# One-core transformer blocks on Trainium2: the recurrence's gates in three fp32r passes, its two directions at two places of a head

## The chip, the cores and the metric

The kernel runs on one NeuronCore of a Trainium2 chip. The engines meant here are TensorE (PE, matmuls), VectorE (DVE), ScalarE (ACT, with function tables that an ACT_TABLE_LOAD exchanges) and SyncE (SP, which issues the DMAs). Each works off its own queue of instructions in order; semaphores make one wait for another. The metric is the device time of one launch in microseconds, smaller is better.

## What is computed

Two transformer blocks follow each other. The first (a gated delta rule, a spatial gating and a mixture of experts) is not touched. The second mixes tokens by grouped-query attention and, beside it, by a bidirectional gated linear recurrence, both over 512 tokens and 16 meta tokens (528 columns); gates of tanh form weigh the two and are added, and a feed-forward layer follows. The part that the change concerns is the recurrence, here for one direction:

```python
def rg_lru(xc, wa, ba, wx, bx, lam, reverse):
    xb = xc.reshape(B, T, RNN_BLOCKS, RNN_BLOCK)          # 8 blocks of 128 channels
    r = sigmoid(einsum('btnc,ncd->btnd', xb, wa) + ba)
    i = sigmoid(einsum('btnc,ncd->btnd', xb, wx) + bx)
    log_a = RG_C * r * log_sigmoid(lam)
    a = exp(log_a)
    u = sqrt(-expm1(2.0 * log_a)) * (i * xc)
    # h[t] = a[t] * h[t-1] + u[t], backwards in time if reverse
```

`xc` is a projection of the tokens after a convolution over four of them. So for each block of 128 channels there are four products of a 128x128 weight with 528 columns: two gates, `rg` and `ig`, in two directions `d`.

## The kernel before

The second block's loop (L1552 on) runs over eight heads `n`, and in each it computes attention head `n` and the recurrence's block `n` together. A head has these pieces, written as generators of which `next` runs one stage:

- `gates` (L2028): three dense products of 128 channels by 512 tokens into a `psA` buffer, 24 matmuls of 128x512 each, called ga, rn and gr here after what they write (ga and rn by a tanh, gr as the GELU factors `grx`, `gry`).
- `attention`: the weights of four query tiles, two at a time, each six matmuls of 264 columns into a `psD` buffer; DVE's maximum `m` (TENSOR_REDUCE), ACT's exponential `pr` with its sum `s`, DVE's normalisation (L2111); then `turned` transposes two tiles on PE: 16 columns into a free part of the same `psD` buffers (L2117), 512 into `psB` (L2122), split into `PThi` by ACT and `PTlo` by DVE. The product with the values comes a head later (`next(a0)`) and gives `ao`.
- `rnn_x` (L1984): 48 matmuls of 264 columns for the next head's projection `xr`, and its convolution `xc` on DVE. It also issues the DMAs of the gates' weights `wg`, one head ahead.
- `rnn_gates` (L2013): the four products in fp32, eight matmuls of 264 columns (L2023) into `psD` tiles, a sigmoid of ACT each, and `ig*xc` on DVE (L2026).
- `rnn`: of the head before, on ACT and DVE only: `th` (tanh, then `th<-a,th` of DVE, L2069), the exponential of `rg`, a square root, `ig<-ig,th` (L2075) and the scan (L2078) for each direction, then the sum of the directions and `ao`.

An fp32 matmul shows as two records in the trace, one in the format fp32r as one. The dense products, weights and projections already use three fp32r passes (`mm3`, L190 to L192): a value is split into a high part, rounded to fp32r by an ACT copy, and the rest, by a DVE subtraction (`split`, L162), and high by high, high by rest and rest by high are added up. Their columns are read `by_turns`: a half's columns are taken from its first and second half alternately, and `unturned` when the result is read.

PE's order is that of the code, by hand (L1549). The tile scheduler orders ACT's and DVE's instructions, and their order is fixed in the built program. In heads 1 to 6 PE's order is: ga, the product with the values of the head before, the gates of both directions, weights of tiles 0 and 1, rn, `turned`, gr, weights of tiles 2 and 3, `rnn_x` of the next head, `turned`. In head 7 the product with the values stands between the two directions. PSUM holds two buffers each of `psA`, `psB` and `psD`; gates and attention weights share `psD`. The pool of `rg`, `ig`, `xr`, `xc` and `wg` has two buffers of each; the scans of head n-1 run during head n, ahead of the gates of n+1, which take over their `rg` buffer.

Of the kernel before, what the change touches and what calls it, by code (L numbers as in the profile page):

```python
# [9 lines left out]
FT = mybir.dt.float32  # L10
FR = mybir.dt.float32r
I32 = mybir.dt.int32
BF = mybir.dt.bfloat16
AF = mybir.ActivationFunctionType
# [44 lines left out]
def by_turns(x):  # L59

    return x.rearrange("p (s c) -> p c s", s=2)
# [14 lines left out]
class Net:  # L76
# [1443 lines left out]
    def block2(self, rctx, pctx):  # L1520
        nc, I = self.nc, self.I
        T = META + S
        h = self.res
        octx = ExitStack()
        self.wraw = self.pool(octx, "wraw", 4, side="right")
        bp = self.pool(octx, "b2c", side="right")
        self.h2_d = self.dr.tile([NT, 128, D], FT, name="h2_d")
        self.q_d = self.dr.tile([NH, 128, S], FT, name="q_d")
        with ExitStack() as ctx:
            gp = self.pool(ctx, "kv", side="right")  # L1530
            kv = self.kv_tiles(gp)
            xctx = ctx.enter_context(ExitStack())
            xp = self.pool(xctx, "xn", side="right")
            xT = (xp.tile([128, NK, T], FR, name="xn_hi"), xp.tile([128, NK, T], FR, name="xn_lo"))
            with ExitStack() as c:
                vec, cl = self.vec2, self.cl
                self.norm_kvq(c, h, xT, kv, gp)
            rctx.close()
            ga, rn = ([gp.tile([128, S], FT, name=f"{m}{n}") for n in range(NK)] for m in ("ga", "rn"))
            self.whl = self.pool(xctx, "whl", 2, side="right")  # L1540
            pctx.close()
            pctx = ExitStack()
            self.psums(pctx, 2, 2, 2)
            w_out = I["w_out_2"][0]
            mix = []
            with ExitStack() as c:
                rp = self.pool(c, "rnl", 2)
                tp = self.pool(c, "atl", 2)
                c.enter_context(self.tc.manual_schedule(engines={mybir.EngineType.PE}))  # L1549
                x = self.rnn_x(rp, 0, vec, xT)  # L1550
                a0 = st0 = old = None
                for n in range(NK):  # L1552
                    a = self.attention(tp, n, kv, rn, ga, gp, mix)
                    g = self.gates(rp, n, xT, rn, ga)
                    if n + 1 < NK:
                        next(g)
                        if n:
                            next(a0)
                        st = self.rnn_gates(rp, n, vec, x)
                        if old:  # L1560
                            next(old)
                        next(g)
                        next(a)
                        next(g)
                        next(a)
                        next(g)
                        if n:
                            r0 = self.rnn(rp, n - 1, cl, st0, rn)
                            next(r0)
                        next(a)  # L1570
                        if n + 1 < NK:
                            x = self.rnn_x(rp, n + 1, vec, xT)
                        next(g)
                        if n + 1 < NK:
                            next(a)
                        if n:
                            next(r0)
                            old = a0
                    else:
                        next(g)  # L1580
                        st = self.rnn_gates(rp, n, vec, x, lambda: next(a0))
                        next(old)
                        next(g)
                        next(a)
                        next(g)
                        next(a)
                        if n:
                            r0 = self.rnn(rp, n - 1, cl, st0, rn)
                            next(r0)
                        next(a)  # L1590
                        next(g)
                        next(g)
                        if n + 1 < NK:
                            x = self.rnn_x(rp, n + 1, vec, xT)
                        if n + 1 < NK:
                            next(a)
                        if n:
                            next(r0)
                        if n:
                            next(a0)  # L1600
                    a0, st0 = a, st
                for _ in self.rnn(rp, n, cl, st, rn):
                    pass
                pd = None
                pss = []
                for k in range(0, NK, 2):
                    if k == 2:
                        next(a0)
                        next(a0)
                    hi, lo = self.wchunk(w_out, k * 128, 2, 0, 512)  # L1610
                    if k == 0:
                        next(a0)
                        for _ in range(2):
                            pd = self.psD.tile([128, 2, 512], FT, name="psD")
                            pss += [pd[:, 0, :], pd[:, 1, :]]
                    for t in range(NT):
                        self.tm_step(pss[t], hi, lo, mix, k, TOKS[t], NK)
            xctx.close()
            h = self.pool(octx, "hB").tile([128, NT, D], FT, name="hB")
            for t in range(NT):  # L1620
                nc.sync.dma_start(h[:, t, :], self.h2_d[t])
            for t in range(NT):
                nc.vector.tensor_tensor(h[:, t, :512], h[:, t, :512], pss[t], OP.add)
            pctx.close()
            hT, first = self.mix_out(octx, ctx, mix, h)
        with ExitStack() as ctx:
            self.ffn(ctx, h, hT, first)
        octx.close()
# [353 lines left out]
    def rnn_x(self, p, n, vec, xT):  # L1982

        nc, I = self.nc, self.I  # L1984
        T = META + S
        H = T // 2
        nhi, nlo = xT
        wg = p.tile([128, 2, 2, 128], FT, name="wg")
        nc.sync.dma_start(wg[:, 0], I["rg_wa_2"][0, :, n].rearrange("d c e -> c d e"))
        nc.sync.dma_start(wg[:, 1], I["rg_wx_2"][0, :, n].rearrange("d c e -> c d e"))  # L1990
        hi, lo = self.wchunk(I["w_in_2"][0], 0, NK, 1536 + n * 128, 128)
        xr = p.tile([128, T + 3], FT, name="xr")
        nc.vector.memset(xr[:, 0:2], 0.0)
        nc.vector.memset(xr[:, T + 2:], 0.0)
        for j in range(2):
            js = slice(j * H, (j + 1) * H)
            ps = self.psA.tile([128, 512], FT, name="psA")
            for k in range(NK):
                self.mm3(ps[:, :H], hi[:, k, :], lo[:, k, :], by_turns(nhi[:, k, js]), by_turns(nlo[:, k, js]),
                         k == 0, k == NK - 1)  # L2000
            self.act(halves(xr[:, 2 + j * H:2 + (j + 1) * H]), unturned(ps[:, :H]), AF.Copy)
        c = p.tile([128, T], FT, name="xc")
        nc.vector.tensor_scalar(c, xr[:, 0:T], vec[:, n:n + 1], vec[:, 32 + n:33 + n], op0=OP.mult, op1=OP.add)
        for j in range(1, 4):
            nc.vector.scalar_tensor_tensor(c, xr[:, j:j + T], vec[:, 8 * j + n:8 * j + n + 1], c,  # L2005
                                           op0=OP.mult, op1=OP.add)
        return c, wg

    def rnn_gates(self, p, n, vec, x, meanwhile=lambda: None):

        nc = self.nc
        T = META + S
        H = T // 2  # L2013
        c, wg = x
        rg = p.tile([128, 2, T], FT, name="rg")
        ig = p.tile([128, 2, T], FT, name="ig")
        for d in range(2):
            if d:
                meanwhile()
            for w, dst, bias in ((0, rg, 40), (1, ig, 56)):  # L2020
                ps = self.psD.tile([128, 2, 512], FT, name="psD")
                for j in range(2):
                    nc.tensor.matmul(ps[:, j, :H], wg[:, w, d, :], c[:, j * H:(j + 1) * H], start=True, stop=True)  # L2023
                self.act(dst[:, d, :].rearrange("p (a b) -> p a b", a=2), ps[:, :, :H], AF.Sigmoid,
                         bias=vec[:, bias + 8 * d + n:bias + 8 * d + n + 1])
        nc.vector.tensor_tensor(ig, ig, c[:, None, :].to_broadcast([128, 2, T]), OP.mult)  # L2026
        return rg, ig

    def gates(self, p, n, xT, rn, ga):

# [279 lines left out]
```

## Time and profile before

| | |
|---|---|
| time, median of three runs | 1963.28 us (1961.18 to 1964.82) |
| profiled run, time / span | 1958.82 / 1957.0 us |
| mean granted clock of TensorE | 0.977 |
| busy, share of span: PE / DVE / ACT | 1804.4 (92%) / 994.8 (51%) / 706.7 (36%) |
| the eight heads' loop: first weights of head 0 to those of head 7 | 1292.86 to 1534.75 us |

The shares are means over the two blocks and the experts; what a change in the heads' loop is worth is read there, from the timeline of each engine. In a timeline row stand the start, the busy time, engine, line, operation, output and inputs, shapes and the count of like instructions that the row joins; in brackets the idle time ahead of it and what ended that.

### The profile page before, as it was taken

To read this page: it belongs to the slowest core of one execution; us is meant where nothing else is said; L and a number is where in the kernel's file an instruction comes from. 1 tells how busy PE (TensorE), PEld (TensorE's weight loads), DVE (VectorE), ACT (ScalarE), POOL (GpSimd) and SP (SyncE) were. 2 spreads that over 40 slices of the span, in tenths; PEclk is the share of its full clock that TensorE was granted. 3 is DMA by queue.
4 is the path that set the end of the run, shared out by engine and by line. 5 is a ranking of instruction groups with operands and counts; after the bars stand their busy time and mean duration, and the time that the engine had idled before them with its cause. 6 is when DMAs were issued, how large, how long until landed. Compare 5 with 4: busy or idle time off the path is not lost. (4 is left out here: it accounts for less than half of the span.)

```text
span 1957.0 us, 23667 instructions
## 1 busy us (share of the span) xinstructions
PE 1804.4 (92%) x9193; PEld 1340.7 (69%) x9193; DVE 994.8 (51%) x1856; ACT 706.7 (36%) x1156; POOL 18.7 (1%) x30
## 2 busy tenths in 40 slices
PE   6899899879999879998889887999999999999999
PEld 5787578767889733443333334888888778888887
DVE  6743577763546622222212238756887863333333
ACT  5232443423333512111101016456767743323332
POOL 0000000000000000000000000000000000000000
PEclk9899999999999979999999998999999999999999
DMA  8636767596558499999999975332221243333231
GB/s 257 97 88 114 107 76 86 119 159 95 98 179 303 176 412 425 426 425 425 425 425 426 376 307 186 119 119 71 81 75 55 66 128 97 97 107 98 98 129 65
DMA packets 255716, 372.64 MB, mean 190 GB/s; under 512 B 30386, under 2 KB 196819, under 8 KB 231667
## 3 DMA queue, kind: packets, MB, share of 16 engines
q1 hardware_dynamic: 245666, 345.94, 56.7%
q10 hardware_dynamic: 7632, 16.78, 2.2%
q0 software_dynamic: 2304, 8.39, 1.1%
q8 instruction: 73, 1.20, 0.2%
q14 instruction: 41, 0.33, 0.1%
HBM read 349.03 MB, written 22.04 MB: 190 GB/s over the span
## 5 line engine op out<-in xcount | busy, mean ns | idle before, releaser
L90 ACT ACTIVATE whi<-raw 128x1024 fp32r<-128x1024 f32 (+1 forms) x203 | 234.2, 1158 | 470.3 <-PE psA L191 291.0
L162 DVE TENSOR_TENSOR wlo<-raw,whi 128x1024 fp32r<-128x1024 f32 (+1 forms) x195 | 249.0, 1278 | 256.9 <-ACT whi L90 239.9
L1267 PE MATMUL psB<-mwt,XT 128*64 128x512 f32 x1008 | 234.5, 600 | 15.0 <-ACT XT L90 9.0
L192 PE MATMUL psA<-hT_hi,wlo 128*128 128x512 f32 (+1 forms) x456 | 177.7, 390 | 16.4 <-DVE wlo L162 16.4
L1267 PEld LDWEIGHTS psB<-mwt,XT 128*64 128x64 f32 x1008 | 74.0, 138 | 163.3 <-issue 137.9
L190 PE MATMUL psA<-hT_hi,whi 128*128 128x512 f32 (+1 forms) x456 | 178.4, 391 | 0.9 <-ACT whi L90 0.9
L191 PE MATMUL psA<-hT_lo,whi 128*128 128x512 f32 (+1 forms) x456 | 178.4, 391 | 0.0
L1332 DVE TENSOR_TENSOR res<-res,psA 128x512 f32<-128x512 f32 x128 | 79.3, 679 | 115.2 <-PE psA L1327 115.2
L1300 PE MATMUL psB<-mwt,hbT 128*64 128x512 f32 x480 | 117.1, 596 | 21.5 <-DMA mwt<-in_w 20.1
L191 PE MATMUL psA<-hn_lo,whi 128*128 128x512 f32 (+1 forms) x368 | 136.3, 370 | 0.3 <-DVE hn_lo L2174 0.3
L190 PE MATMUL psA<-hn_hi,whi 128*128 128x512 f32 (+1 forms) x368 | 136.4, 371 | 0.2 <-ACT hn_hi L90 0.2
L192 PE MATMUL psA<-hn_hi,wlo 128*128 128x512 f32 (+1 forms) x368 | 136.2, 370 | 0.0
L1276 DVE TENSOR_TENSOR sl<-sl,psB 128x512 f32<-128x512 f32 x16 | 11.0, 688 | 204.8 <-PE psB L1267 204.8
L190 PE MATMUL psA<-xn_hi,whi 128*128 128x512 f32 (+1 forms) x320 | 109.4, 342 | 0.4 <-ACT qx L90 0.4
L192 PEld LDWEIGHTS psA<-hT_hi,wlo 128*128 128x128 f32 (+1 forms) x456 | 87.0, 191 | 32.2 <-DVE wlo L162 18.2
L192 PE MATMUL psA<-xn_hi,wlo 128*128 128x512 f32 (+1 forms) x320 | 108.2, 338 | 0.0
L191 PE MATMUL psA<-xn_lo,whi 128*128 128x512 f32 (+1 forms) x320 | 108.1, 338 | 0.0
L1300 PEld LDWEIGHTS psB<-mwt,hbT 128*64 128x64 f32 x480 | 36.2, 136 | 96.7 <-issue 57.4
L191 PEld LDWEIGHTS psA<-hT_lo,whi 128*128 128x128 f32 (+1 forms) x456 | 87.1, 191 | 20.4 <-issue 8.4
L190 PEld LDWEIGHTS psA<-hT_hi,whi 128*128 128x128 f32 (+1 forms) x456 | 87.3, 191 | 17.3 <-issue 3.4
L90 ACT ACTIVATE hbT<-psA 128x512 f32<-128x512 f32 x16 | 9.6, 597 | 238.8 <-PE psA L1284 238.8
L190 PEld LDWEIGHTS psA<-hn_hi,whi 128*128 128x128 f32 x368 | 69.5, 189 | 9.5 <-ACT hn_hi L90 0.5
(569 smaller groups left out, 3459.8 us busy)
## 6 DMA issues: line engine op xcount, KB each, us to landing
mwt<-in_w SPq DMA_DIRECT2D x188, 1024.0 KB, 20.7
raw<-in_w_in SPq DMA_DIRECT2D x108, 512.0 KB, 7.6
raw<-in_w_ffn_in SPq DMA_DIRECT2D x44, 512.0 KB, 3.9
raw<-in_w_ffn_out SPq DMA_DIRECT2D x22, 512.0 KB, 3.6
raw<-in_w_pa SPq DMA_DIRECT2D x8, 512.0 KB, 4.2
raw<-in_w_pb SPq DMA_DIRECT2D x8, 512.0 KB, 4.2
raw<-in_w_o SPq DMA_DIRECT2D x8, 512.0 KB, 6.9
raw<-in_w_out SPq DMA_DIRECT2D x8, 512.0 KB, 3.6
```

The source lines that it names most:

```text
L90: ins = self.nc.scalar.activation(out, in_, func, **kw)
L162: self.nc.vector.tensor_tensor(lo, x, hi.bitcast(FT), OP.subtract)
L190: nc.tensor.matmul(out, whi, xhi, start=first, stop=False)
L191: nc.tensor.matmul(out, whi, xlo, start=False, stop=False)
L192: nc.tensor.matmul(out, wlo, xhi, start=False, stop=last)
L1267: nc.tensor.matmul(ps[CAP * i:CAP * (i + 1), :], XT[:, r0 + k, CAP * i:CAP * (i + 1)], w_, start=(r0 + k == 0), stop=(r0 + k == NK - 1))
L1276: nc.vector.tensor_tensor(so, so, h[1], OP.mult)
L1300: nc.tensor.matmul(pys[half][CAP * i:CAP * (i + 1), :], hT[:, r0 + k, CAP * i:CAP * (i + 1)], ws[i][:, k, half * 512:(half + 1) * 512], st ...
L1332: nc.vector.tensor_tensor(x, x, unturned(ps), OP.add)
```

## The change

`rnn_x` now splits the gates' weights (`wghi`, and the rest into a buffer of `wg`) and the convolved columns (the high part into an `xr` buffer, the rest `xclo`): two more ACT copies and two more DVE subtractions in a head. `rnn_gates` becomes a generator: each product is three fp32r passes on columns by turns, 24 matmuls of 264 columns a head in place of eight in fp32, and the sigmoid puts the columns back in order. Its first stage, direction 0, stays where the gates stood. Its second, direction 1 with the multiplication by `xc`, moves in heads 0 to 6 behind `turned` of tiles 0 and 1 and ahead of gr. In head 7 the order stays. `xc`, `wghi` and `xclo` get one buffer each. Lines below L2000 move by up to 12.

```diff
--- before.py
+++ after.py
@@ -1556,13 +1556,15 @@
                         next(g)
                         if n:
                             next(a0)
-                        st = self.rnn_gates(rp, n, vec, x)
+                        rg = self.rnn_gates(rp, n, vec, x)
+                        st = next(rg)
                         if old:
                             next(old)
                         next(g)
                         next(a)
                         next(g)
                         next(a)
+                        next(rg)
                         next(g)
                         if n:
                             r0 = self.rnn(rp, n - 1, cl, st0, rn)
@@ -1578,7 +1580,10 @@
                             old = a0
                     else:
                         next(g)
-                        st = self.rnn_gates(rp, n, vec, x, lambda: next(a0))
+                        rg = self.rnn_gates(rp, n, vec, x)
+                        st = next(rg)
+                        next(a0)
+                        next(rg)
                         next(old)
                         next(g)
                         next(a)
@@ -1988,6 +1993,8 @@
         wg = p.tile([128, 2, 2, 128], FT, name="wg")
         nc.sync.dma_start(wg[:, 0], I["rg_wa_2"][0, :, n].rearrange("d c e -> c d e"))
         nc.sync.dma_start(wg[:, 1], I["rg_wx_2"][0, :, n].rearrange("d c e -> c d e"))
+        ws = p.tile([128, 2, 2, 128], FR, name="wghi", bufs=1), p.tile([128, 2, 2, 128], FR, name="wg")
+        self.split(*ws, wg)
         hi, lo = self.wchunk(I["w_in_2"][0], 0, NK, 1536 + n * 128, 128)
         xr = p.tile([128, T + 3], FT, name="xr")
         nc.vector.memset(xr[:, 0:2], 0.0)
@@ -1999,32 +2006,37 @@
                 self.mm3(ps[:, :H], hi[:, k, :], lo[:, k, :], by_turns(nhi[:, k, js]), by_turns(nlo[:, k, js]),
                          k == 0, k == NK - 1)
             self.act(halves(xr[:, 2 + j * H:2 + (j + 1) * H]), unturned(ps[:, :H]), AF.Copy)
-        c = p.tile([128, T], FT, name="xc")
+        c = p.tile([128, T], FT, name="xc", bufs=1)
         nc.vector.tensor_scalar(c, xr[:, 0:T], vec[:, n:n + 1], vec[:, 32 + n:33 + n], op0=OP.mult, op1=OP.add)
         for j in range(1, 4):
             nc.vector.scalar_tensor_tensor(c, xr[:, j:j + T], vec[:, 8 * j + n:8 * j + n + 1], c,
                                            op0=OP.mult, op1=OP.add)
-        return c, wg
-
-    def rnn_gates(self, p, n, vec, x, meanwhile=lambda: None):
+        cs = p.tile([128, T + 3], FR, name="xr")[:, 0:T], p.tile([128, T], FR, name="xclo", bufs=1)
+        self.split(*cs, c)
+        return c, cs, ws
+
+    def rnn_gates(self, p, n, vec, x):
 
         nc = self.nc
         T = META + S
         H = T // 2
-        c, wg = x
+        c, (chi, clo), (whi, wlo) = x
         rg = p.tile([128, 2, T], FT, name="rg")
         ig = p.tile([128, 2, T], FT, name="ig")
         for d in range(2):
-            if d:
-                meanwhile()
             for w, dst, bias in ((0, rg, 40), (1, ig, 56)):
                 ps = self.psD.tile([128, 2, 512], FT, name="psD")
                 for j in range(2):
-                    nc.tensor.matmul(ps[:, j, :H], wg[:, w, d, :], c[:, j * H:(j + 1) * H], start=True, stop=True)
-                self.act(dst[:, d, :].rearrange("p (a b) -> p a b", a=2), ps[:, :, :H], AF.Sigmoid,
+                    js = slice(j * H, (j + 1) * H)
+                    self.mm3(ps[:, j, :H], whi[:, w, d, :], wlo[:, w, d, :], by_turns(chi[:, js]), by_turns(clo[:, js]),
+                             True, True)
+                self.act(dst[:, d, :].rearrange("p (a s c) -> p a s c", a=2, s=2),
+                         ps[:, :, :H].rearrange("p a (c s) -> p a s c", s=2), AF.Sigmoid,
                          bias=vec[:, bias + 8 * d + n:bias + 8 * d + n + 1])
+            if d == 0:
+                yield rg, ig
         nc.vector.tensor_tensor(ig, ig, c[:, None, :].to_broadcast([128, 2, T]), OP.mult)
-        return rg, ig
+        yield
 
     def gates(self, p, n, xT, rn, ga):
 
```

ACT in a head, from the end of rn to grx, before (`th`, `rg`, `a` belong to `rnn`; `whi` is a weight's high part):

```order
L90 ACTIVATE rn_8942<-psA 128x512
L90 ACTIVATE PThi<-psD 16x128 x2
L90 ACTIVATE PThi<-psB 128x4x128 x2
L90 ACTIVATE th<-rg,cl 128x528
L90 ACTIVATE rg<-rg,cl 128x528
L90 ACTIVATE th<-rg,cl 128x528
L90 ACTIVATE a_9878<-rg 128x528
L90 ACTIVATE rg<-rg,cl 128x528
L90 ACTIVATE a_9883<-rg 128x528
L90 ACTIVATE whi<-raw 128x1024
L90 ACTIVATE grx<-psA 128x512
```

And after:

```order
L90 ACTIVATE rn_8942<-psA 128x512
L90 ACTIVATE PThi<-psD 16x128 x2
L90 ACTIVATE PThi<-psB 128x4x128 x2
L90 ACT_TABLE_LOAD
L90 ACTIVATE rg<-psD,vec_5881 128x528
L90 ACTIVATE ig<-psD,vec_5881 128x528
L90 ACTIVATE th<-rg,cl 128x528
L90 ACTIVATE wghi<-wg 128x512
L90 ACT_TABLE_LOAD
L90 ACTIVATE rg<-rg,cl 128x528
L90 ACTIVATE th<-rg,cl 128x528
L90 ACTIVATE grx<-psA 128x512
```

Direction 1's sigmoids with two table loads and the weights' copy came in; the squares `a`, one `rg` exponential and `whi` moved behind grx.

DVE in the softmax of tiles 2 and 3, from a reduction on, before:

```order
L2103 TENSOR_REDUCE m<-psD 128x1
L162 TENSOR_TENSOR wlo<-raw,whi 128x1024
L2104 SCALAR_TENSOR_TENSOR m<-m,qs 128x1
L2103 TENSOR_REDUCE m<-psD 128x1
L2048 TENSOR_SCALAR gry<-gry 128x512
L2109 RECIPROCAL s<-s 128x1
L2104 SCALAR_TENSOR_TENSOR m<-m,qs 128x1
L2049 TENSOR_TENSOR gry<-gry,grx 128x512
L2111 TENSOR_SCALAR pr<-pr,s 128x528
L2109 RECIPROCAL s<-s 128x1
L162 TENSOR_TENSOR qlo<-qf,qhi 128x512
L2111 TENSOR_SCALAR pr<-pr,s 128x528
```

After, where the first reduction and `gry<-gry` stand ahead of the piece:

```order
L2116 SCALAR_TENSOR_TENSOR m<-m,qs 128x1
L2081 SCALAR_TENSOR_TENSOR th<-a_9950,th 128x528
L2115 TENSOR_REDUCE m<-psD 128x1
L2061 TENSOR_TENSOR gry<-gry,grx 128x512
L2121 RECIPROCAL s<-s 128x1
L2081 SCALAR_TENSOR_TENSOR th<-a_9955,th 128x528
L2123 TENSOR_SCALAR pr<-pr,s 128x528
L2116 SCALAR_TENSOR_TENSOR m<-m,qs 128x1
L162 TENSOR_TENSOR wlo<-raw,whi 128x1024
L162 TENSOR_TENSOR qlo<-qf,qhi 128x512
L2121 RECIPROCAL s<-s 128x1
L2123 TENSOR_SCALAR pr<-pr,s 128x528
```

The two `th<-a,th`, which stood ahead of the first reduction, now stand between the two normalisations' inputs.

DVE around the scans (printed as SCALAR_TENSOR_TENSOR `th<-rg,ig`), before:

```order
L162 TENSOR_TENSOR PTlo<-psB,PThi 128x4x128
L2005 SCALAR_TENSOR_TENSOR xc<-xr,vec_5881,xc 128x528
L162 TENSOR_TENSOR PTlo<-psB,PThi 128x4x128
L2078 SCALAR_TENSOR_TENSOR th<-rg,ig 128x528 x2
L162 TENSOR_TENSOR wlo<-raw,whi 128x1024
L2080 TENSOR_TENSOR th<-th 128x512
L162 TENSOR_TENSOR wlo<-raw,whi 128x1024
```

And after:

```order
L162 TENSOR_TENSOR PTlo<-psB,PThi 128x4x128
L2012 SCALAR_TENSOR_TENSOR xc<-xr,vec_5881,xc 128x528
L162 TENSOR_TENSOR PTlo<-psB,PThi 128x4x128
L2090 SCALAR_TENSOR_TENSOR th<-rg,ig 128x528
L162 TENSOR_TENSOR xclo<-xc,xr 128x528
L2087 TENSOR_TENSOR ig<-ig,th 128x528
L162 TENSOR_TENSOR wlo<-raw,whi 128x1024
L2090 SCALAR_TENSOR_TENSOR th<-rg,ig 128x528
L162 TENSOR_TENSOR wlo<-raw,whi 128x1024
L2092 TENSOR_TENSOR th<-th 128x512
```

Three instructions now stand between the scans: the new `xclo`, the second direction's `ig<-ig,th`, and one `wlo`.

## Rows read from the trace of the kernel before

**Rows 1.** Windows, one head each: length, busy us of each engine, granted clock.

```profile
core 0: us, PE busy (x) PEld busy (x) DVE busy (x) ACT busy (x) POOL busy (x), PEclk, DMA share, GB/s
1326.80:1361.70 34.90, 33.82 (x196) 29.23 (x196) 27.68 (x51) 25.68 (x45) 0.00 (x0) 1.00 0.24 71
1396.39:1431.09 34.70, 33.61 (x196) 29.16 (x196) 27.77 (x52) 25.54 (x45) 0.00 (x0) 1.00 0.27 76
1500.46:1534.75 34.29, 33.45 (x196) 29.32 (x196) 26.85 (x49) 24.91 (x44) 0.00 (x0) 1.00 0.19 57
```

**Rows 2.** Waits in the loop: waiter, releaser, us in total, times, longest.

```profile
ACT L90 <- DVE th L2078: 9.6, 6, 1.7
...
PEld psD L190 <- ACT rg L90: 8.5, 8, 1.4
```

**Rows 3.** Timeline of PE, one head.

```profile
1396.39 0.38 PE L190 MATMUL psD<-kThi,qhi 128*128 128x264 f32 x1 [0.95 <-ACT rg L90]
...
1397.84 0.38 PE L190 MATMUL psA<-xn_hi,whi 128*128 128x512 f32 x1
...
1403.02 0.67 PE L2117 MATMUL psD<-ident,pr 128*16 128x128 f32 x2
...
1404.32 0.46 PE L190 MATMUL psA<-xn_hi,whi 128*128 128x512 f32 x1
...
1409.58 0.28 PE L190 MATMUL psD<-kThi,qhi 128*128 128x264 f32 x1
...
1410.93 0.28 PE L190 MATMUL psA<-xn_hi,whi 128*128 128x264 f32 x1
...
1416.33 0.38 PE L2117 MATMUL psD<-ident,pr 128*16 128x128 f32 x2
...
1426.23 3.89 PE L2023 MATMUL psD<-xc,wg 128*128 128x264 f32 x16
```

**Rows 4.** Timeline of ACT, the same head.

```profile
1403.05 1.06 ACT L90 ACTIVATE whi<-raw 128x1024 fp32r<-128x1024 f32 x1 [0.51 <-ACT pr L90]
...
1415.43 1.28 ACT L90 ACT_TABLE_LOAD   x1
1416.72 1.18 ACT L90 ACTIVATE th<-th 128x528 f32<-128x528 f32 x2
...
1425.20 1.28 ACT L90 ACT_TABLE_LOAD   x1 [1.56 <-DVE th L2078]
1427.32 0.70 ACT L90 ACTIVATE rg<-psD,vec 128x528 f32<-128x528 f32 x1 [0.83 <-PE psD L2023]
```

**Rows 5.** Timeline of DVE, the same head.

```profile
1405.29 0.47 DVE L162 TENSOR_TENSOR PTlo<-psD,PThi 16x128 fp32r<-16x128 f32 x2
...
1410.55 0.70 DVE L2103 TENSOR_REDUCE m<-psD 128x1 f32<-128x528 f32 x1
...
1415.31 0.49 DVE L2111 TENSOR_SCALAR pr<-pr,s 128x528 f32<-128x528 f32 x1
...
1417.40 1.33 DVE L2075 TENSOR_TENSOR ig<-ig,th 128x528 f32<-128x528 f32 x2 [0.28 <-ACT th L90]
...
1422.74 2.38 DVE L2078 TENSOR_TENSOR_SCAN th<-rg,ig 128x528 f32<-128x528 f32 x2
```

**Rows 6.** Groups of DVE in that head: count, busy us, mean ns, idle ahead.

```profile
L162 DVE TENSOR_TENSOR wlo<-raw,whi 128x1024 fp32r<-128x1024 f32 x4 | 4.8, 1208 | 0.9 <-PE psB L2122 0.9
...
L2069 DVE SCALAR_TENSOR_TENSOR th<-a,th 128x528 f32<-128x528 f32 x2 | 1.4, 709 | 2.3 <-ACT a L90 2.3
```

**Rows 7.** Timeline of PE, the last head and the layer behind.

```profile
1544.16 0.35 PE L190 MATMUL psD<-kThi,qhi 128*128 128x264 f32 x1 [1.22 <-DVE PTlo L162]
...
1583.09 0.79 PE L190 MATMUL psD<-whi,ga 128*128 128x512 f32 x1 [2.02 <-ACT ga L90]
```

**Rows 8.** Timeline of ACT and PE, the first head.

```profile
1288.87 1.28 ACT L90 ACT_TABLE_LOAD   x1
...
1292.86 0.38 PE L190 MATMUL psD<-kThi,qhi 128*128 128x264 f32 x1
```

## The prediction

> **What bounds the kernel now.** Only the second block's loop over eight heads is touched, so the view of windows comes first, one window a head. A head is counted from W, its first attention-weight matmul, to the next head's W: 34.70 us, of which TensorE (PE) is busy for 33.61, VectorE (DVE) for 27.77 and ScalarE (ACT) for 25.54, at a granted clock of 1.00 [rows 1]. PE hardly rests, so fewer PE microseconds look like a gain. The waits tell another story: PE waits for ACT's sigmoid of the gate `rg` ahead of W, and ACT's table load ahead of that sigmoid waits six times for DVE's scan [rows 2]. So a second chain runs round the head, as long as PE's own: DVE's scans, ACT's table load, sigmoid, attention weights, softmax, scans again. A change has to be walked along both.
>
> The marks, from the timelines. S is the start of the third query tile's weights. Before, W to S is 1396.39 to 1409.58, 13.19 us: weights 1.45, the dense product for `rn` 5.18, `turned` 1.30, the dense product for `gr` 5.26 [rows 3]. S to the next W (1431.09) is 21.51 us, and PE starts the gates 16.65 us after S (1426.23) [rows 1, 3].
>
> **What the change takes off PE.** The eight fp32 matmuls of the gates are 16 records of 3.89 us with the last one's drain; 16 starts 0.221 apart are 3.54 us of PE. In their place stand 24 matmuls of the shape of the attention weights, of which twelve take 1.45 us (1396.39 to 1397.84, first one slower) or 1.35 (1409.58 to 1410.93 by twelve steps of 0.112) [rows 3]. That is 2.68 us, a saving of 0.86 us a head, 6.9 us for eight. This is the sum if PE alone counted.
>
> **First half of the head, W to S.** The second direction's twelve matmuls now stand between `turned` and the dense product for `gr`. They write `psD`, which has two buffers, and both hold the two attention tiles in whose spare columns `turned` has just put its 16-column transposes. These are read last by DVE's `PTlo<-psD`, queued behind `wlo`, which needs ACT's `whi` copy, which starts only when `rn`'s dense product ends: copy at 1403.05, `PTlo` pair at 1405.29 of 0.47 us, so 1405.61 with its pass to PE [rows 4, 5]. `rn`'s product ended at 1403.02 and the transposes at 1404.32: PE would now stand still for 1.30 us where it ran straight on [rows 3]. That such a wait comes is seen in the last head, where weights already follow `turned` directly and PE waits 1.22 us for `PTlo` [rows 7]. New W to S: 1.45 + 5.18 + 2.60 + 1.45 + 5.26 = 15.94, plus 2.74. ACT must do what the order shows in that time: after the `PThi` copies end (9.4 us after W) two table loads of 1.28, two sigmoids, a tanh, an exponential and the like, some 6.2 us in all by the rows of these kinds [rows 4]. It is done 15.6 us after W; `grx` can start 0.2 after S, at 16.1. That hides, by half a microsecond.
>
> **Second half, S to W.** On DVE the chain runs from the third tile's `TENSOR_REDUCE` (0.97 us after S) to the fourth tile's normalisation (1415.31, 5.73 after S), then to `ig<-ig,th` (1417.40, 7.82 after S) and to the end of the second scan (1425.12, 15.54 after S) [rows 5]. The change puts three groups into this queue.
> - The two `th<-a,th` operations, before ahead of S and in ACT's shadow, now stand inside the softmax: 0.709 each by their record [rows 6], 0.62 start to start, so some 1.3 us. PE's next transposes wait 0.73 for that (normalisation ends 7.5 after S, PE is there at 6.75).
> - They push `ig<-ig,th` to 9.0 after S, by 1.2; the sqrt path on ACT comes out there too.
> - Between the two scans now stand `xclo` (0.62 as a 528-column subtraction, as the other 528-column operations) and one `wlo` (1.21 by its record, 1.12 start to start) [rows 6]. The second `ig<-ig,th` only changes place.
>
> End of the second scan: 15.54 + 1.2 + 0.62 + 1.12 = 18.5, I take 18.4. The table load ahead of the `rg` sigmoid waits for exactly this scan, as it did before (scan end 1425.12, load 1425.20), because the new `rg` takes the buffer that the scan reads; the change leaves that buffer count alone. Then 0.08 + load 1.28 + sigmoid 0.70 + 0.06: W falls 20.54 after S [rows 4]. PE alone would be ready earlier: gates at 16.65 + 0.73 = 17.38, W at 17.38 + 1.64 = 19.02 (six matmuls 0.67, drain 0.21, sigmoid 0.70, hand-over 0.06). So DVE's chain still ends last, now by 1.5 us, and the 0.86 us saved on PE is not seen. Against 21.51 the half gains 0.97, since the second direction and the `ao` copy that stood between the first sigmoid and W are gone from there.
>
> **Head by head.** Steady head: 15.94 + 20.54 = 36.48 against 34.70, so +1.8. The first W comes about 0.8 earlier, as one direction with two split copies takes the place of two fp32 directions between 1288.87 and 1292.86 [rows 8]. Head 0 to 1, where no scans run yet, is PE's path: 15.94 + 16.65 + 1.64 = 34.23 against 33.94 (1292.86 to 1326.80), +0.3. Head 1 to 2: 36.48 against 34.90, +1.6. Four heads of +1.8: +7.2. Head 6 to 7, where both directions stay before W and the `ao` copy stays between their sigmoids: second scan at 17.8, `ao` 20.9, W 22.2 after S, so 38.1 against 34.29, +3.8 [rows 1]. Sum -0.8 + 0.3 + 1.6 + 7.2 + 3.8 = **+12.1 us**. Nothing outside the loop changes; the last head's own work and what follows shift with it. The profiled run took 1958.82 and would take 1970.9; it lies 4.46 below the median of 1963.28, which makes **1975**.
>
> **Rivals.**
> - *PE's path decides.* The second scan ends by 16.9 after S (the `th` operations fit into gaps, or the load is not held). Then S to W is 19.02 and a steady head 34.96, +0.3; with -0.8, +0.3, 0 for head 1 to 2, five times nearly +0.3 and about +1.0 at the end this is +1.9 in all: 1965. For it: PE's busy share [rows 1]. Against it: the load's wait for the scan in six of the heads [rows 2].
> - *The other side, faster.* `PTlo<-psD` is done when PE gets there, within 1.30 us of `rn`'s end instead of 2.59, and the scan isn't last. A steady head is then 1.30 shorter, seven heads 9.1: 1956, near the 6.9 us of PE work. The point that decides is whether `wlo` stands ahead of `PTlo` in DVE's queue; in the order it does, and the last head shows the wait at 1.22 [rows 7].
> - *A table switch costs more than its record.* The trace shows none of that: one load starts 0.08 after the scan that it waits for, and of another, 1415.43 to 1416.71, the next activation starts 0.01 behind [rows 4]. If the two loads that are new in the first half each cost one more length of 1.28, ACT would be 2.56 later there, less the half microsecond of margin, and `gry` in DVE's queue would push the whole second half: 2.1 for each of seven heads, +14.5, 1990. The Trainium skill ("ScalarE: Activation LUTs", What ACT_TABLE_LOAD costs) gives 1283 ns for the load and some 1380 ns more for a drain; the trace agrees with the first and shows no second. Its section on table sets, the hidden batching unit, asks for calls to be grouped by set, which this change undoes; here the records price that, and they are the price taken above.
> - *The clock.* A PE pause of 2.02 us near 1583 is followed by a 128x512 matmul of 0.79, where 0.38 was such a one's record [rows 3, 7]; the pauses foreseen are 1.3 and 1.5 to 1.7 us. Should they lower it too, a head loses several microseconds: beyond 1985.
>
> **How the numbers follow.** Measuring can tell about 0.2% of this kernel, 3.9 us, from no change: faster is below 1959.4, slower above 1967.2. The forecast (1969 to 1983 with its own slips of half a microsecond to one on each head) has 0.66, PE's path 0.14, the faster case 0.09, the dearer switch 0.05, the clock 0.04; the 0.02 left lies between forecast and PE's path and counts as no change. So faster 0.09, within 0.16, slower 0.75. The range takes in PE's path at its low end and stops short of the dear switch: 1963 to 1984.
>
> **What would show it.** Right: steady heads of 36 to 37 us; a PE wait of 1.3 us for `PTlo` ahead of the first `psD<-xr,wghi` matmul after `turned`; PE's wait for the `rg` sigmoid ahead of W grown from 0.95 to some 1.7; the table load ahead of that sigmoid still released by the scan, whose end lies 18 to 19 us after S; two more table loads a head of 1.28 with no gap behind. Wrong: a W without a wait for `rg`, heads of 35 us or less, a scan that ends before 17 after S, or gates that PE starts with the psD buffers already free.

## The result and the profile after

The changed kernel takes 1975.16 us (median of four runs, 1972.43 to 1976.88) against 1962.23 for the kernel before: a ratio of 1.0061 with a 95% interval of 1.0043 to 1.0079, so 0.6% slower. The forecast was 1975. In the profiled runs the spans are 1970.6 and 1957.0 us.

The page of the changed kernel, shares of the span by engine:

```profile
span 1970.6 us, 23847 instructions
...
PE 1799.1 (91%) x9257; PEld 1341.7 (68%) x9257; DVE 1003.1 (51%) x1872; ACT 730.9 (37%) x1186; POOL 18.6 (1%) x30
```

PE has 5.3 us less to do than before and the kernel is 13.6 us longer. The windows of the heads, as in [rows 1] (length, busy time of PE, its weight loads, DVE, ACT and POOL, granted clock):

```profile
1292.49:1326.70 34.21, 32.66 (x204) 29.23 (x204) 22.25 (x43) 22.39 (x39) 0.00 (x0) 1.00 0.34 102
1326.70:1363.01 36.31, 32.82 (x204) 29.16 (x204) 26.88 (x48) 28.49 (x48) 0.00 (x0) 1.00 0.21 61
1399.31:1435.61 36.30, 32.98 (x203) 29.10 (x204) 28.77 (x54) 29.04 (x49) 0.00 (x0) 1.00 0.25 73
1508.22:1546.50 38.28, 34.84 (x215) 30.52 (x216) 30.34 (x56) 30.33 (x51) 0.00 (x0) 1.00 0.22 69
```

A steady head grew from 34.70 to 36.30 us, the one before the last from 34.29 to 38.28. The timeline of PE in a steady head, against [rows 3]:

```profile
1399.31 0.38 PE L190 MATMUL psD<-kThi,qhi 128*128 128x264 f32 x1 [1.62 <-ACT rg L90]
...
1406.63 0.27 PE L2129 MATMUL psD<-ident,pr 128*16 128x128 f32 x1 [0.41 <-DVE pr L2123]
...
1408.63 0.35 PE L190 MATMUL psD<-xr,wghi 128*128 128x264 f32 x1 [0.85 <-DVE PTlo L162]
...
1415.23 0.28 PE L190 MATMUL psD<-kThi,qhi 128*128 128x264 f32 x1
...
1432.49 0.28 PE L190 MATMUL psD<-xr,wghi 128*128 128x264 f32 x1
...
1435.61 0.38 PE L190 MATMUL psD<-kThi,qhi 128*128 128x264 f32 x1 [1.61 <-ACT rg L90]
```

From W, a head's first attention-weight matmul, to S, the first one of its third query tile, it is 15.92 us (1399.31 to 1415.23), from S to the next W 20.38. PE waits twice on the way to direction 1's first product, 0.41 and 0.85, and 1.6 for the `rg` sigmoid ahead of W, where it waited 0.95 before. The timelines of ACT and DVE ahead of that W, against [rows 4, 5]:

```profile
1433.56 1.28 ACT L90 ACT_TABLE_LOAD   x1 [3.61 <-DVE th L2090]
1434.86 0.70 ACT L90 ACTIVATE rg<-psD,vec 128x528 f32<-128x528 f32 x1
```

```profile
1428.73 1.24 DVE L2090 TENSOR_TENSOR_SCAN th<-rg,ig 128x528 f32<-128x528 f32 x1
1429.89 0.67 DVE L162 TENSOR_TENSOR xclo<-xc,xr 128x528 fp32r<-128x528 f32 x1
1430.49 0.69 DVE L2087 TENSOR_TENSOR ig<-ig,th 128x528 f32<-128x528 f32 x1
1431.11 1.21 DVE L162 TENSOR_TENSOR wlo<-raw,whi 128x1024 fp32r<-128x1024 f32 x1
1432.25 1.24 DVE L2090 TENSOR_TENSOR_SCAN th<-rg,ig 128x528 f32<-128x528 f32 x1
```

The chain reads off these rows: `xclo`, `ig` and `wlo` stand between the scans, the second scan ends at 1433.49, the load starts 0.07 later, the sigmoid follows the load, and W follows the sigmoid. PE began the product for that sigmoid at 1432.49; six matmuls and their drain are some 0.9 us by the prediction's rows, so it was ready while the load still ran.

### The profile page after: what moved, and what is told of

The parts are those of the page before. It is cut to its first block, busy times and chain, and to the rows that moved or that the text cites. A ratio compares the mean times of both kernels' runs of the same rounds, so it can differ in the third digit from the quotient of the medians.

```text
span 1970.6 us, 23847 instructions
## 1 busy us (share of the span) xinstructions
PE 1799.1 (91%) x9257; PEld 1341.7 (68%) x9257; DVE 1003.1 (51%) x1872; ACT 730.9 (37%) x1186; POOL 18.6 (1%) x30
```

## The experiments

The theory was that a head lasts as long as PE's stretch from W to S and then DVE's and ACT's chain from S to W. The rivals: PE's work counts; the place alone, the splits alone or the wait for `PTlo` alone makes the loss. The table has what the traces show in a steady head, in us; ratios are those of the runs' medians to the kernel before, run beside them, with their interval. That kernel took 1964.92 us beside runs 1 to 4, 1961.57 beside 5 to 8 and 1961.24 beside 9 and 10.

| kernel | W to S | S to W | head | ratio to before |
|---|---|---|---|---|
| before | 13.19 | 21.51 | 34.70 | 1 |
| the change | 15.92 | 20.38 | 36.30 | 1.0061 [1.0043, 1.0079] |
| 1: direction 1 put back | 13.19, three times 14.59 | 22.11, three times 22.39 | 35.30, three times 36.98 | 1.0030 [1.0009, 1.0050] |
| 2: place alone, fp32 | 16.36 | 19.82 | 36.18 | 1.0049 [1.0035, 1.0063] |
| 3: three `rg` buffers | 17.08 | 18.88 | 35.96 | 1.0054 [1.0034, 1.0073] |
| 4: direction 1 behind gr | 17.5 to 18.5 | 21.2 to 21.4 | 38.8 to 39.7 | 1.0135 [1.0097, 1.0173] |
| 5: early table load | 16.07 | 19.10 | 35.16 | 1.0021 [1.0009, 1.0033] |
| 6: put back, copy of `ao` behind | 14.45 | 20.02 | 34.47 | 0.9994 [0.9986, 1.0003] |
| 7: before, copy of `ao` behind | 14.09 | 20.45 | 34.54 | 0.9997 [0.9986, 1.0007] |
| 8: as 6, tanh for the sigmoids | 13.34 | 21.36 | 34.70 | 1.0041 [1.0026, 1.0055] |
| 9: three passes, order freed | 12.91 | 20.30 | 33.21 | 0.9952 [0.9935, 0.9970] |
| 10: fp32, order freed | 13.12 | 20.45 | 33.57 | 0.9958 [0.9944, 0.9972] |
| 11: the change, columns first | 15.80 | 24.89 | 40.70 | a single run, 1998.27 us |

**1. Direction 1 put back.** In the changed kernel:

```diff
                         st = next(rg)
+                        next(rg)
...
                         next(a)
-                        next(rg)
                         next(g)
```

> The changed kernel with direction 1 put back directly behind direction 0; the three passes and the splits stay. Ring theory (a head is PE's stretch from W to S, then the chain of DVE and ACT from S to the next W): W to S falls back to 13.2 us, since no gates and no wait for PTlo stand there; the second scan ends 0.6 later than before (xclo in front of it), so that ao, its copy on ACT and the rg sigmoid of direction 1 come 0.6 later: S to W 22.1, a steady head 35.3 against 34.7 before and 36.3 with the change; about 1966 us. Rival, PE's work counts: 0.86 us less a head than before, 33.8 a head, 1955 us. Rival, the splits are what costs: as slow as the change, 36.3 a head.

One steady head (W at 1405.40) is what was worked out, 13.19 + 22.11 = 35.30. So the passes and splits alone, without the new place, cost 0.6 us a head: `xclo` delays the second scan, the scan `ao`, and `ao` the sigmoid of direction 1, whose place in ACT's queue is behind `ao`'s copy. Three others take 36.98, with the same chain but another clock. Windows of W to S, first of such a head, then of the one of 35.30:

```profile
1440.70:1455.30 14.60, 14.60 (x71) 12.88 (x72) 8.15 (x17) 10.49 (x20) 0.00 (x0) 0.88 0.23 67
...
1405.40:1418.60 13.20, 13.08 (x71) 11.45 (x72) 8.15 (x17) 10.77 (x20) 0.00 (x0) 1.00 0.25 74
```

The granted clock is 0.88 in the longer one. PE stood still for 2.2 us ahead of each, and in the longer one the matmuls soon come 0.22 us apart instead of 0.11: the lower of the clock's two levels, for some microseconds. The ratio of this run holds such heads, so the price of the passes and splits is read from the head at 1.00.

```profile
1440.70 0.38 PE L190 MATMUL psD<-kThi,qhi 128*128 128x264 f32 x1 [2.21 <-ACT rg L90]
...
1441.37 0.28 PE L192 MATMUL psD<-kThi,qlo 128*128 128x264 f32 x1
...
1441.65 0.43 PE L191 MATMUL psD<-kTlo,qhi 128*128 128x264 f32 x1
1441.88 0.43 PE L192 MATMUL psD<-kThi,qlo 128*128 128x264 f32 x1
```

**2. The place alone.** The kernel before with `rnn_gates` as a generator and the order of the change, but fp32 products and no splits:

```diff
+            if d == 0:
+                yield rg, ig
```

> The kernel before with only the place of direction 1 changed: fp32 products as before, no splits. Ring theory: the wait for PTlo of 1.3 us and 1.8 us of fp32 products come into W to S, 16.35 us; in S to W the scan ends near 16.7 after S, so W falls 18.9 after S and a steady head is 35.2 us, 0.5 more than before; with a dearer last head about 1967 us. Rival, the place alone makes the whole loss: 36.3 a head, 1975 us. Rival, PE's work counts: same PE work as before, 34.7 a head, 1963 us.

W to S came out as worked out (16.36), S to W 0.92 us longer (19.82 for 18.9). So the rival came true: the place alone makes nearly the whole loss, 36.18 against 36.30 with passes and splits. The step that was missed, in ACT's timeline:

```profile
1430.70 1.28 ACT L90 ACT_TABLE_LOAD   x1 [3.66 <-PE psD L2026]
1432.00 0.70 ACT L90 ACTIVATE rg<-psD,vec 128x528 f32<-128x528 f32 x1
```

Here the load waits for PE's product (begun 1429.58), though the scan ended 1.2 us earlier, so the whole 1.28 us lies behind PE. By the semaphores in the traces, ACT waits ahead of this load for both DVE and PE; in the kernel before and in the changed one it waits there for DVE alone, and the sigmoid behind the load waits for PE.

**3. Three `rg` buffers.**

```diff
-        rg = p.tile([128, 2, T], FT, name="rg")
+        rg = p.tile([128, 2, T], FT, name="rg", bufs=3)
```

> The changed kernel with a third buffer for rg (grx and gry give one each), so that the table load and the sigmoid ahead of W no longer wait for the second scan; the order of DVE and ACT in a head stays nearly the same. If this wait alone is what ends last: S to W falls from 20.4 to 18.8, 1.6 us less in each of five heads, 1967 us. Ring theory with a second hold behind it: ao and the reductions of tiles 0 and 1 still stand behind the scan on DVE, so the normalised weights come late for the transposes and W to S grows by about 1 us: a steady head about 35.6 to 35.7, some 3 to 4 us less in all, 1971 us.

To make room, `grx` and `gry` have one buffer each in this run. W comes 1.5 us earlier after S, and W to S gives 1.16 of it back. What is left, 0.34 us a head, the times can't tell from the change (1.0054 and 1.0061), the less as the head before the last is 1.16 us longer here. DVE still runs scan, `wlo`, `ao` and only then the maxima, so that the normalised weights are late for the transposes on PE:

```profile
1408.69 0.27 PE L2129 MATMUL psD<-ident,pr 128*16 128x128 f32 x1 [1.25 <-ACT pr L90]
1409.47 0.27 PE L2129 MATMUL psD<-ident,pr 128*16 128x128 f32 x1 [0.51 <-DVE pr L2123]
```

**4. Direction 1 behind gr.** `next(rg)` one line further down.

> The changed kernel with direction 1 behind gr in place of ahead of it, so that psD has long been freed when PE comes to its matmuls. If the wait for PTlo is what the change costs: 1.3 us less a head, 35.0 us, 1966 us. Ring theory: the two table loads and the sigmoids then stand between grx and the exponentials of tiles 2 and 3 on ACT, and weights of tile 2 must wait for the rg sigmoid to free psD; W to S about 16.3, and the softmax, the scans and W come later after S: a steady head of 37 us or more, slower than the change, about 1980 us or above.

Slower than the change by 2.5 to 3.4 us a steady head, as the theory said. W to S was foreseen at 16.3 and is 17.5 to 18.5: PE now waits 2.61 us at S for the `rg` sigmoid, which frees `psD`:

```profile
1426.43 0.38 PE L190 MATMUL psD<-kThi,qhi 128*128 128x264 f32 x1 [2.61 <-ACT rg L90]
```

**5. The early table load.** In the changed kernel's `rnn`, behind the square roots:

```diff
+        e = p.tile([128, 1], FT, name="early", bufs=1)
+        self.act(e, cl[:, 0, n:n + 1], AF.Sigmoid)
```

> The changed kernel with one sigmoid of a single column behind the square roots, so that the table load for the gates' sigmoid runs while ACT is idle and no longer behind the second scan; the rest of ACT's and DVE's order in a head stays. If scan, load, sigmoid and W are the only chain: W falls 1.28 earlier, 35.0 a head, some 8 us less in all. With the second hold that the third rg buffer showed (ao and the reductions of tiles 0 and 1 stand behind the scan on DVE and then feed the exponentials): W to S grows by about what S to W loses, and a head comes out near the 35.96 of the run with three rg buffers, some 2 us less in all.

S to W is 19.10, shorter by 1.28. Of ACT's rows, the load now stands in a gap:

```profile
1394.08 1.28 ACT L90 ACT_TABLE_LOAD   x1
1395.37 0.20 ACT L90 ACTIVATE early<-cl 128x1 f32<-128x1 f32 x1
...
1401.61 0.70 ACT L90 ACTIVATE rg<-psD,vec 128x528 f32<-128x528 f32 x1 [3.60 <-DVE th L2092]
```

The second hold that was expected behind it cost 0.15 us in W to S, where run 3 lost 1.16: in this build DVE has the first maximum ahead of `ao`'s last addition, in run 3 behind it. With 35.16 a head the load's place is worth 1.14 us, of the 1.60 that the change costs. In the kernel before, the load waits for the same scan and isn't on the path: the sigmoid behind it waits 0.83 us more for PE's product [rows 4], and W hangs on the sigmoid of direction 1, behind `ao`'s copy. The change took that copy out from ahead of W, and so the load came onto the path.

**6, 7. The copy of `ao` behind the sigmoids,** on run 1 and on the kernel before. In `attention`, for the first half of `self.split(*mix[h], o)`:

```diff
+        ins = nc.scalar.activation(mhi, o, AF.Copy)
+        self.tc.add_manual_dep(ins.ins, self.last_act.name, ...
```

> Three passes and splits, both directions at the old place, and ACT's copy of ao put behind the four sigmoids in place of between direction 0 and 1. Chain theory: W no longer waits for ao; the gates run at PE's and the sigmoids' pace, 16.65 + two times (0.67 + 0.21 + 0.70 + 0.06) = 19.9 after S, W to S 13.2 to 13.7, a steady head 33.2 to 33.7, 1 to 1.5 us under before: about 1955 us for a before of 1964. Rival, ao is needed at once anyway (its reductions' place on DVE): a head of 34.5 or more, no faster than before.

> The kernel before with that one order alone: ACT's copy of ao behind the four sigmoids; fp32 products. Chain theory: 16.65 + two times (0.88 + 0.21 + 0.70 + 0.06) = 20.3 after S against 21.5, W to S 13.2 to 13.6, a steady head 33.5 to 33.9, about 1957 us: most of the gain of the run with three passes is then this order and not the passes, whose share is about 0.4 us a head. Rival, PE's work counts: 0.9 us a head between the two.

S to W falls as worked out, to 20.02 and 20.45. W to S rises to 14.45 and 14.09 (13.73 and 13.49 where no scans run yet), so a head gains 0.2 us on before and the times show nothing. The 13.2 to 13.7 foreseen for W to S was missed in the heads with scans, and the rival of run 6 (34.5 a head) came true. DVE's timeline of run 6 behind W (1429.62) has the hold:

```profile
1430.27 0.68 DVE L162 TENSOR_TENSOR wg<-wg,wghi 128x512 fp32r<-128x512 f32 x1
...
1430.87 1.24 DVE L2038 TENSOR_TENSOR ig<-ig,xc 128x1056 f32<-128x1056 f32 x1
1432.04 0.67 DVE L2161 TENSOR_TENSOR rn<-ao,ga 128x512 fp32r<-128x512 f32 x1
1432.64 1.30 DVE L2115 TENSOR_REDUCE m<-psD 128x1 f32<-128x528 f32 x2
```

The low part of the weights, the multiplication by `xc` and the low part of `ao`, three operations that nobody waits for soon, stand ahead of the maxima that PE's transposes wait for.

**8. Tanh for the sigmoids,** with halves in the scales and biases behind and a one-column tanh behind the square roots.

```diff
-... AF.Sigmoid,
+... AF.Tanh, scale=0.5,
```

> As the run before the last (three passes, old place, copy of ao behind), with the sigmoids written as 0.5 + 0.5 tanh(x/2), whose halves go into the scales and biases that follow, and a tanh of one column behind the square roots: two table loads a head in place of three, both where ACT is idle. The exponentials of tiles 0 and 1 then no longer wait for a load of 1.28. If that load is on the path, W to S falls to 13.2 and a head to 33.1; if PE alone bounds the head by then, no more than 0.3 us a head, 2 us in all, under the run without tanh.

W to S is 13.34, near what was said; but the scheduler put both scans ahead of `xc` and `PTlo` here, and the product with the values waits for that, so S to W is 21.36 and the forecast of 33.1 a head was missed. The run says little on the loads.

```profile
1428.47 0.48 PE L190 MATMUL psB<-PThi,v_hi 16*128 16x512 f32 x1 [1.04 <-DVE PTlo L162]
```

**9, 10. The order freed,** with three passes and with fp32. Beside the edit of 6, the last head has its product with the values ahead of both directions, ACT's `wghi` stands behind the sigmoids (in 9), and DVE's operations that nobody waits for soon stand behind the maxima. From the edit of 10:

```diff
-                        st = self.rnn_gates(rp, n, vec, x)
+                        rg = self.rnn_gates(rp, n, vec, x)
+                        st = next(rg)
+                        next(g)
+                        next(a)
                         if old:
                             next(old)
-                        next(g)
-                        next(a)
+                        next(rg)
...
+        ins = nc.vector.tensor_tensor(ig, ig, c[:, None, :].to_broadcast([128, 2, T]), OP.mult)
+        self.tc.add_manual_dep(ins.ins, self.last_m.name, ...
```

> Three passes and splits, both directions at the old place in every head (in the last one behind the product with the values), and what stood between scan and softmax put behind: ACT's copies of ao and of the weights behind the four sigmoids, DVE's multiplication by xc and the low parts of ao and of the weights behind the maxima of tiles 0 and 1. If these holds are what keeps PE's saving from showing: W to S 13.2, S to W 20.0 as in the run with the copy behind, 33.2 a head against 34.7 before, seven heads 232 to 234 against 241.9, some 8 to 10 us less: about 1953 for a before of 1962. Rival, another hold of DVE comes out behind: 34 us a head or more, 4 us less at most.

> The same order with the fp32 products of before, without splits. W to S 13.2, S to W 20.45 as in the run of before with the copy behind, 33.65 a head, seven heads 235 to 237: some 5 to 6.5 us less than before. The difference to the run with three passes is then what the passes are worth where PE bounds the head: 0.4 us a head, 3 us in all, and not the 0.86 of PE's work, since the hand-overs between product and sigmoid stay. Rival, PE's work counts in full there: 0.86 a head, 6 us in all between the two. Rival, the splits eat the passes: no difference.

Both are some 0.4 to 0.5% faster than before: 1952.87 and 1954.05 against 1961.24 us. The intervals of the two ratios overlap, so the times can't tell what the passes are worth. The windows of a steady head can, 9 then 10, and both heads are near what was worked out (33.2 and 33.65):

```profile
1394.61:1427.82 33.21, 32.69 (x204) 29.26 (x204) 28.90 (x54) 26.55 (x47) 0.00 (x0) 1.00 0.27 80
```

```profile
1396.96:1430.53 33.57, 33.57 (x196) 29.29 (x196) 27.89 (x54) 25.62 (x44) 0.00 (x0) 1.00 0.27 79
```

In 10 PE is busy without a gap. In 9 it has 0.88 us less to do, the 0.86 of the prediction, and 0.36 of that shows (0.4 was expected), since PE then waits for a sigmoid between the directions:

```profile
1392.87 0.38 PE L190 MATMUL psD<-xr,wghi 128*128 128x264 f32 x1 [0.40 <-ACT rg L90]
```

DVE's rows of 9, with the maxima first and the rest behind:

```profile
1395.59 1.38 DVE L2123 TENSOR_REDUCE m<-psD 128x1 f32<-128x528 f32 x2 [0.17 <-PE psD L192]
1396.89 0.15 DVE L2124 SCALAR_TENSOR_TENSOR m<-m,qs 128x1 f32<-128x1 f32 x1
1396.95 0.68 DVE L2002 TENSOR_TENSOR wg<-wg,wghi 128x512 fp32r<-128x512 f32 x1
1397.55 0.15 DVE L2124 SCALAR_TENSOR_TENSOR m<-m,qs 128x1 f32<-128x1 f32 x1
1397.62 1.25 DVE L2043 TENSOR_TENSOR ig<-ig,xc 128x1056 f32<-128x1056 f32 x1
...
1400.71 0.68 DVE L2169 TENSOR_TENSOR rn<-ao,ga 128x512 fp32r<-128x512 f32 x1
```

**11. The transposed columns first.** In the changed kernel the copies and subtractions of `PThi` and `PTlo` from `psD` are ordered ahead of gr's `whi` and `wlo`.

```diff
+            for ins, first in zip(self.two, self.hold):
+                self.tc.add_manual_dep(ins, first.name, ...
```

> The changed kernel with the copies and subtractions of the 16 transposed columns (PThi, PTlo from psD) put ahead of gr's whi and wlo on ACT and DVE, so that psD comes free earlier; the scheduler also moves the scans ahead of xc in the other half, so only W to S is compared. If the wait for PTlo is a cost of DVE's order alone: direction 1 starts 1 us earlier and W to S falls from 15.9 to 14.8. If what counts is that gr's weights can only be split from rn's end on: psD is free earlier, but PE then waits about as long for wlo at gr's third matmul, and W to S stays at 15.7 to 16.0.

W to S is 15.80. The wait for `PTlo` is gone, and PE waits for `wlo` at gr's third matmul instead:

```profile
1380.35 0.48 PE L198 MATMUL psA<-xn_hi,wlo 128*128 128x512 f32 x1 [0.56 <-DVE wlo L162]
```

In both orders the copies and subtractions start when `rn` ends, and W to S differs by 0.12 us. So their order isn't what makes the stretch long. In the other half (24.89) the scans came ahead of `xc`, as in run 8, and PE waits there for a weight's `whi` and `wlo` as well; as the text ahead of the run says, it isn't part of the comparison.

## Why the prediction held, step by step

- **PE's saving isn't seen:** held. 0.86 us a head was the price, 0.88 the measure (33.57 less 32.69 in runs 10 and 9), and the steady head grew by 1.60.
- **W to S, 15.94:** measured 15.92. The wait of 1.30 came in two pieces, 0.41 and 0.85. `ao`'s low part `rn<-ao,ga` now stands between the maxima and their scaling (`m<-m,qs`), so the table load for the exponentials starts 3.50 us after W in place of 3.20 (1402.81 here, 1399.59 before), and PE waits for the second tile's normalisation first. The end is the same, since `whi` starts when `rn` ends, and `wlo` and `PTlo` follow it as foreseen:

```profile
1401.98 0.68 DVE L162 TENSOR_TENSOR rn<-ao,ga 128x512 fp32r<-128x512 f32 x1
...
1407.07 1.23 DVE L162 TENSOR_TENSOR wlo<-raw,whi 128x1024 fp32r<-128x1024 f32 x1 [0.58 <-ACT whi L90]
1408.21 0.47 DVE L162 TENSOR_TENSOR PTlo<-psD,PThi 16x128 fp32r<-16x128 f32 x2
```

- **ACT's cover of half a microsecond:** 0.23 us by the idle time ahead of `grx`. It held, with less to spare:

```profile
1414.48 0.72 ACT L90 ACTIVATE th<-rg,cl 128x528 f32<-128x528 f32 x1
1415.43 0.60 ACT L90 ACTIVATE grx<-psA 128x512 f32<-128x512 f32 x1 [0.23 <-PE psA L192]
```

- **S to W, 20.54:** 20.38. The second scan ended 18.26 after S (18.4 forecast), and load, sigmoid and hand-over took the 2.12 of the forecast. The two `th<-a,th` cost less than priced: PE's transposes waited 0.44 for the normalisation and not 0.73, and `ig<-ig,th` started 8.78 after S and not 9.0.
- **Head by head:** first W -0.7 against the same matmul ahead of the loop (-0.8 forecast), head 0 to 1 +0.27 (+0.3), 1 to 2 +1.41 (+1.6), the four steady ones +6.45 (+7.2), 6 to 7 +3.99 (+3.8). That is +11.4 for +12.1. Each steady head was priced 0.2 too dear, most of it in the second scan's end.
- **"Nothing outside the loop changes":** not quite. The span grew by 13.6. Of the 2.2 us beyond the loop some 1.4 lie behind the pause of 2.02 us that [rows 7] show near 1583. The pause is the same in both, but the low clock behind it lasts longer: granted clock over 6.63 us from the pause's end, after and then before:

```profile
1594.87:1601.50 6.63, 6.63 (x18) 5.30 (x19) 3.43 (x4) 2.00 (x2) 0.00 (x0) 0.57 0.94 316
```

```profile
1583.09:1589.72 6.63, 6.63 (x24) 5.61 (x25) 4.32 (x5) 2.00 (x2) 0.00 (x0) 0.78 0.96 326
```

Why it lasts longer in one execution than in the other wasn't tried. That 1975 and 1975.16 lie so close is luck: 0.7 us too much in the loop, 2.2 us beyond it that weren't foreseen, and a profiled run that lies 2.73 us under its median where 4.46 were taken nearly cancel.

- **The rivals.** PE's path deciding fell: in all five heads from 1 on W waits for the sigmoid behind the scan. The faster case fell at the point named for it, `wlo` ahead of `PTlo`; run 11 shows that removing that point wouldn't have made it true. The dearer switch fell: where the load left the chain (run 5), S to W lost 1.28, the length of its record. The Trainium skill ("ScalarE: Activation LUTs", What ACT_TABLE_LOAD costs) gives that and some 1.38 for a drain; no run here shows a drain. The clock rival didn't come true in the change, with pauses ahead of W up to 1.76 us; it did in run 1, with pauses of 2.2, at 1.4 to 1.7 us a head and not the several that the prediction feared. In the sum of PE's path the prediction counts the steady heads five times where there are four; that is 0.3 us and leaves the 1965 as it is.
- **What the prediction didn't separate.** It laid 0.62 + 1.12 us on what stands between the scans and 2.74 on the new place of direction 1. The runs say that place and splits don't add up: the place alone +1.5 (run 2), passes and splits alone +0.6 (run 1), both +1.6. In run 2 the load waits for the product, in the change for the scan; one of two holds ends last in each, and their prices overlap.

## What to carry to other kernels

When an engine is 97% busy inside a loop, walk the second chain round the loop before pricing a saving on the first: here 0.86 us of matmuls a head turned into 1.6 us of loss, because a moved step put a wait for a PSUM buffer, a table load that had been off the path and queued DVE operations into a chain of equal length. Write down for every instruction that lands in an in-order queue who waits behind it; taking the operations that nobody awaits soon (low parts, a copy for later) out from ahead of the sigmoids and of a reduction gave 7 to 8 us, with fp32 products and with three passes, where the copy alone gave nothing that the times show. And put a table load where its engine idles, by a one-column call of the coming function, since a load can sit behind the very wait that its function has.

## What the chip showed that was not expected

A table load doesn't always start as early as it could. In run 2 it started only when the matmul that its sigmoid reads was done, with 1.28 us added to the path; in the change and before it waited for the scan that frees the sigmoid's buffer; in run 5 a call of one column ahead moved it into a gap of ACT.

PE pauses of 2.1 to 2.2 us ahead of W were followed by the lower clock level in three of five heads of run 1, with 1.4 to 1.7 us lost each, and in the other two the granted clock stayed at 1.00. A shorter pause was followed by it too, and not each time. Ahead of the first W the changed kernel's PE paused for 1.76 us, and the granted clock of that head was 1.00. Runs 4 and 5 have the same pause at the same place (1.76 and 1.75 us), and there the granted clock was 0.63 and 0.62 over the next 4.5 us, with W to S 1.6 to 1.7 us longer than in the next head. In run 4, of two like pauses of 2.61 us, one was followed by a granted clock of 0.92 up to W and one by 1.00. So a wait can cost more than its length.
